# Moving a tiny memory-to-memory transfer from ScalarE's queue into the queue of the loads

## The chip, the cores and the metric

The kernel runs on one core of a Trainium2 chip. The metric is the device time of one execution in microseconds; for the kernel before it is the median of three executions. The profile is a separate execution, and its span runs from the first to the last instruction, so it is a little shorter than the device time. PE is TensorE (PEld its weight loads), DVE is VectorE, ACT is ScalarE, POOL is GpSimd, and SP is SyncE. A name with a q behind it (SPq, ACTq) is that engine issuing a DMA transfer.

## What is computed

```python
def setup_inputs():
    batch, m, k, n = 16, 512, 1024, 768
    return {
        "x": np.random.randn(batch, m, k).astype(np.float32),
        "weight": np.random.randn(k, n).astype(np.float32),
        "sub_value": np.random.randn(batch, m, n).astype(np.float32),
    }

def reference(x, weight, sub_value):
    return (np.matmul(x, weight) - sub_value).astype(np.float32)
```

Batch and m together are 8192 rows, in 64 tiles of 128 rows. The kernel reads x (32 MiB), sub_value (24 MiB) and the weights (3 MiB), and writes the output (24 MiB).

## The kernel before

The kernel is written engine by engine. Each engine has a list of operations (`act.add`, `sp.add`, ...), each with the semaphores that it waits for and the one that it raises; the lists are emitted at the end. For each tile, ScalarE casts x to fp16, TensorE (for most tiles) or VectorE transposes it, ScalarE copies the transposed tile out of PSUM, TensorE multiplies by the weights, and VectorE subtracts sub_value in place, in the ring of buffers from which the output is then stored.

All loads and stores are issued by SP, in a fixed order. A letter names what moves (x, w for weights, s for sub_value, o for output), then come the first tile and the number of tiles:

```python
TRANSFERS = [
    ('x', 0, 1), ('w', 0, 2), ('x', 1, 2), ('w', 2, 2), ('x', 3, 3), ('s', 0, 4),
    ('x', 6, 2), ('x', 8, 4), ('s', 4, 4), ('x', 12, 4), ('s', 8, 8), ('x', 16, 2), ('x', 18, 6), ('s', 16, 8),
    ('x', 24, 8), ('o', 0, 8), ('s', 24, 8), ('x', 32, 8), ('s', 32, 8), ('x', 40, 8),
    # ... cut: the rest alternates in the same way ...
    ('o', 24, 8), ('o', 32, 8), ('s', 56, 8), ('o', 40, 8), ('o', 48, 8), ('o', 56, 5),
    ('o', 61, 2), ('o', 63, 1),
]
```

One more transfer stands outside this list. It copies, from memory to memory, 32 elements (128 bytes) of every 512th row of sub_value into the output, 16 pieces in all. The output's rows are overwritten later by the real stores, so the result does not depend on it. It touches the output's memory early. ScalarE issues it, as the first operation of its list:

```python
    touched = tc.alloc_semaphore("touched")
    act.add(lambda: nc.scalar.dma_start(out=out_flat[:: M_TOT // 16, :Q], in_=sub_flat[:: M_TOT // 16, :Q]), then=(touched, 16))
```

Here `Q` is 32 and `M_TOT` is 8192. The stores wait for it, so that it can't overwrite them, and so in fact does the first of them only (a wait that an engine has made is not repeated):

```python
            if kind == "o":
                waits.append((touched, 16))
                waits.append((counter["finish"], max(finish_at[t] for t in need)))
                # ... cut ...
            sem, value = lane((kind, at))
            # ... cut ...
            if kind == "o":
                here, there = there, here
            sp.add(lambda here=here, there=there: nc.sync.dma_start(out=here, in_=there), waits, (sem, 16))
```

The start of the work, in order, with the parts that the prediction speaks of:

```python
    idle(13)                 # matmuls on zeros, before the first data are there
    cast(0)                  # ACT: waits for x tile 0
    # ... cut: one more idle matmul ...
    transpose_tile(0)        # PE, then ACT copies out of PSUM
    idle(7)
    matmuls(0, 0)            # waits for the first weights, cast by DVE
    matmuls(0, 1)
    idle(2)
    cast(1)
    cast(2)
    # ... cut ...
```

Of the kernel before, what the change touches and what calls it, by code (L numbers as in the profile page):

```python
# [9 lines left out]
Q = 32  # L10
# [94 lines left out]
def kernel(  # L105
# [7 lines left out]
    nc = tc.nc  # L113

    x_flat = x.flatten_outer_dims()
    sub_flat = sub_value.flatten_outer_dims()
    out_flat = out.flatten_outer_dims()

    M_TOT, K = x_flat.shape
# [7 lines left out]
    def view(flat, at, n):  # L127

        first, size = next(one for one in SEGMENTS if one[0] <= at < sum(one))
        assert at + n <= first + size  # L130
        rows = flat[first * P : (first + size) * P].rearrange("(p j) c -> p j c", p=P, j=size)
        return rows[:, at - first : at - first + n]
# [9 lines left out]
    def psum(name, shape, dtype):  # L142
        return ctx.enter_context(nc.psum_tensor(name, shape, dtype)).ap()
# [17 lines left out]
    pt_b = psum("pt_b", [P, NPT, K], F16)  # L161
    po_b = psum("po_b", [P, NPO, 2, 512], F32)

    counter = {}
    for name in ("ident", "idle", "w", "cast", "evac", "pair", "turn", "mul", "finish"):
        counter[name] = tc.alloc_semaphore(name)
# [2 lines left out]
    def count(name):  # L169
        so_far[name] += 1  # L170
        return (counter[name], 1)

    sp, pe = Queue(nc, nc.sync), Queue(nc, nc.tensor)
    act, dve, pool = Queue(nc, nc.scalar), Queue(nc, nc.vector), Queue(nc, nc.gpsimd)

    touched = tc.alloc_semaphore("touched")
    act.add(lambda: nc.scalar.dma_start(out=out_flat[:: M_TOT // 16, :Q], in_=sub_flat[:: M_TOT // 16, :Q]), then=(touched, 16))
    pool.add(lambda: nc.gpsimd.memset(idle_w, 0.0), then=count("idle"))
    pool.add(lambda: nc.gpsimd.memset(idle_x, 0.0), then=count("idle"))  # L179
    dve.add(lambda: nc.vector.memset(ones, 1.0), then=count("ident"))  # L180
# [2 lines left out]
        out=along, data0=ones, data1=ones, initial=0.0, op0=mybir.AluOpType.mult, op1=mybir.AluOpType.add,  # L183
    ), waits=[(counter["ident"], 1)], then=count("ident"))
    dve.add(lambda: nc.vector.transpose(across, along), waits=[(counter["ident"], 3)], then=count("ident"))  # L185
    for a in range(P // Q):
        here = slice(a * Q, (a + 1) * Q)
        dve.add(lambda here=here: nc.vector.tensor_tensor(  # L188
            out=ident[here, here], in0=along[here], in1=across[here], op=mybir.AluOpType.is_equal,
# [41 lines left out]
    def lane(tag):  # L231

        for one in lanes:
            if one["tags"] <= known:
                break
        else:
            one = {"sem": tc.alloc_semaphore(f"lane{len(lanes)}"), "value": 0, "tags": set()}
            lanes.append(one)
        one["value"] += 16
        one["tags"].add(tag)  # L240
        return one["sem"], one["value"]

    def issue():
        nonlocal known, from_w
        while todo:
            kind, at, n = todo[0]
            span = set(range(at, at + n))
            old = {t - NX if kind == "x" else t - NSO for t in span}
            need, by = {
                "w": (set(), "o"),  # L250
                "x": ({t for t in old if t >= 0}, "cast"),
                "s": ({t for t in old if t >= 0}, "o"),
                "o": (span, "finish"),
            }[kind]
            if not need <= done[by]:
                return
            todo.pop(0)
            done[kind] |= span
            if kind == "w":

                first = NSO - 2 * (n_c - at)
                st = so_ring[:, first : first + 2 * n]
                sem, value = lane((kind, at))
                sp.add(lambda st=st, at=at, n=n: nc.sync.dma_start(out=st, in_=w_half[at // n]), then=(sem, 16))  # L264
                for c in range(at, at + n):
                    for r in range(2):
                        here = so_ring[:, first + 2 * (c - at) + r]
                        dve.add(
                            lambda c=c, r=r, here=here: nc.vector.tensor_copy(out=w_sb[:, c, r], in_=here),  # L269
                            waits=[(sem, value)], then=count("w"),  # L270
                        )
                        staged[first + 2 * (c - at) + r] = so_far["w"]
                    w_at[c] = so_far["w"]
                from_w |= {(("w", at), so_far["w"])}
                continue
            ring, size, flat = {
                "x": (x_ring, NX, x_flat), "s": (so_ring, NSO, sub_flat), "o": (so_ring, NSO, out_flat)
            }[kind]
            here = ring[:, at % size : at % size + n]
            there = view(flat, at, n)  # L280
            waits = []
            if kind == "x" and need:
                waits.append((counter["cast"], max(cast_at[t] for t in need)))
                last = max(need, key=lambda t: cast_at[t])
                known |= {tag for t, tag in of_x.items() if t in cast_at and cast_at[t] <= cast_at[last]}
            if kind == "s":
                for t in need:
                    waits.append(landed["o", t])
                    known.add(of_o[t])
                for t in span:  # L290
                    if t % NSO in staged:
                        waits.append((counter["w"], staged.pop(t % NSO)))
                        known |= {tag for tag, value in from_w if value <= waits[-1][1]}
# [3 lines that stand above are left out]
                known |= {of_s[t] for t in finish_at if finish_at[t] <= max(finish_at[u] for u in need)}  # L297
            sem, value = lane((kind, at))
            for t in span:
                landed[kind, t] = (sem, value)  # L300
                {"x": of_x, "s": of_s, "o": of_o}[kind][t] = (kind, at)
            if kind == "o":
                here, there = there, here
            sp.add(lambda here=here, there=there: nc.sync.dma_start(out=here, in_=there), waits, (sem, 16))  # L304

    def cast(mi):
        assert mi in done["x"]
        done["cast"].add(mi)
        x_in = x_ring[:, mi % NX].rearrange("p (g q c r) -> p g c q r", g=2, c=2, r=2)
        first = mi - mi % 2  # L310
        waits = [landed["x", mi]]
        if first in ON_DVE:
            if mi == first:
                b, before = take("x16p", N16P, mi)
                if before is not None:
                    waits.append((counter["pair"], pair_at[before]))
            to = x16p_b[:, slot["x16p", first], mi - first]
        else:
            b, before = take("x16", N16, mi)
            if before is not None:  # L320
                waits.append((counter["turn"], turn_at[before]))
            to = x16_b[:, b]
        to = to.rearrange("p (g c q r) -> p g c q r", g=2, c=2, r=2)
        act.add(lambda: nc.scalar.copy(out=to, in_=x_in), waits, count("cast"))  # L324
        cast_at[mi] = so_far["cast"]
        issue()
# [92 lines left out]
    def finish(mi):  # L419
        assert mi in done["s"]  # L420
        done["finish"].add(mi)
        o = so_ring[:, mi % NSO].rearrange("p (h n) -> p h n", h=2)
        po = po_b[:, slot["po", mi]]
        dve.add(lambda: nc.vector.tensor_tensor(  # L424
            out=o, in0=po[:, :, :NS], in1=o, op=mybir.AluOpType.subtract
        ), [landed["s", mi], (counter["mul"], mul_at[mi])], count("finish"))
        finish_at[mi] = so_far["finish"]
        issue()

    issue()  # L430


# [132 lines left out]
```

## Time and profile before

| | before |
|---|---|
| device time, median of three | 210.57 us (210.28 to 210.61) |
| span of the profiled execution | 208.7 us |
| TensorE busy | 195.2 us (94%) |
| VectorE busy | 127.7 us (61%) |
| ScalarE busy | 113.1 us (54%) |
| bytes moved by DMA | 87.08 MB, 417 GB/s over the span |
| mean granted TensorE clock | 0.993 |

The page cuts the span into 40 slices of about 5.2 us. In the rows of engines and of DMA each digit is the busy share of a slice in tenths, and 9 stands for 90% or more. The row of GB/s says what the DMA engines moved in each slice:

```profile
PEclk9999999999999999999999999999999999999997
GB/s 219 427 426 433 429 433 434 459 426 413 433 466 421 360 438 452 448 408 426 473 408 422 443 419 429 449 438 432 416 454 408 426 452 415 429 438 448 411 412 120
```

In the timeline, a row has the start in us, the duration in us, the engine, the line of the kernel, the operation, and what is written from what; in brackets stands how long the engine had been idle before it and what ended that. A transfer's own row gives the time of its issue on the engine; its time to landing, from issue until its semaphore is complete, stands in the table of transfers.

### The profile page before, as it was taken

The numbers are of one execution on the slowest core, as the hardware profiler recorded it, in microseconds if no ns is written. First come the engines' busy times: TensorE is split into PE (matmuls) and PEld (weight loads), VectorE is DVE, ScalarE is ACT, GpSimd is POOL, SyncE is SP. The second block draws the span as 40 slices with busy tenths as digits, with TensorE's granted clock in tenths as the row PEclk, the third lists the DMA queues.
The fourth block names the chain that finished last, engine by engine and source line by source line (L and its number), as shares of the span: only waits on it lengthen the run. The fifth ranks groups of instructions, "written<-read, shape, count | busy, mean of one in ns | idle before, by whom it ended". The sixth has DMA issues, their size and how long they took to land.

```text
span 208.7 us, 2605 instructions
## 1 busy us (share of the span) xinstructions
PE 195.2 (94%) x1231; PEld 75.4 (36%) x699; DVE 127.7 (61%) x224; ACT 113.1 (54%) x113; POOL 1.0 (0%) x7
## 2 busy tenths in 40 slices
PE   6789799998999999999999999999999999999950
PEld 0133344333434434433442443343344344344310
DVE  2321517945893895597399389479749938942330
ACT  3275678606674761953845676283674747616300
POOL 1000000000000000000000000000000000000000
PEclk9999999999999999999999999999999999999997
DMA  6999999999999999999999999999999999999992
GB/s 219 427 426 433 429 433 434 459 426 413 433 466 421 360 438 452 448 408 426 473 408 422 443 419 429 449 438 432 416 454 408 426 452 415 429 438 448 411 412 120
DMA packets 4932, 87.08 MB, mean 417 GB/s; under 512 B 576, under 2 KB 576, under 8 KB 960
## 3 DMA queue, kind: packets, MB, share of 16 engines
q1 hardware_dynamic: 4896, 87.03, 97.7%
q8 instruction: 1, 0.02, 0.0%
q14 instruction: 3, 0.02, 0.0%
q10 hardware_dynamic: 32, 0.00, 0.0%
HBM read 61.87 MB, written 25.17 MB: 417 GB/s over the span
## 4 chain that ended last, share of the span: by engine, by line
PE 72%; DMA 22%; ACT 2%; issue 1%; DVE 0%; SPq 0%
PE po_b L199 64%; DMA x_ring<-in_x_dram 22%; PE pt_b L342 7%; ACT x_b L324 1%; DVE so_ring L424 0%; ACT xt_b L355 0%; SPq L264 0%; SPq L304 0%; SPq L560 0%; ACT x16p_b L324 0%; SPq L137 0%
## 5 line engine op out<-in xcount | busy, mean ns | idle before, releaser
L199 PE MATMUL po_b<-w_sb,xt_b 128*128 128x384 f16 x704 | 126.0, 326 | 3.2 <-DVE w_sb L269 1.3
L424 DVE TENSOR_TENSOR so_ring<-po_b,so_ring 128x768 f32<-128x768 f32 x64 | 60.5, 956 | 60.0 <-PE po_b L199 38.6
L355 ACT COPY xt_b<-pt_b 128x1024 f16<-128x1024 f16 x44 | 44.5, 1013 | 57.2 <-PE pt_b L342 57.2
L375 DVE STREAM_TRANSPOSE xtp_b<-x16p_b 32x256 f32<-32x256 f32 x144 | 62.7, 435 | 3.5 <-ACT x16p_b L324 1.4
L199 PE MATMUL po_b<-w_sb,xtp_b 128*128 128x384 f16 x320 | 61.4, 326 | 0.5 <-DVE so_ring L424 0.2
L404 PEld LDWEIGHTS <-xt_b 128*128 128x128 f16 x352 | 34.4, 98 | 60.3 <-issue 54.8
L324 ACT CAST x_b<-x_ring 128x1024 f16<-128x1024 f32 x46 | 50.5, 1126 | 9.7 <-DMA x_ring<-in_x_dram 9.7
L342 PE MATMUL pt_b<-ident,x_b 128*128 128x128 f32 x184 | 47.6, 274 | 0.8 <-ACT x_b L324 0.7
L342 PEld LDWEIGHTS pt_b<-ident,x_b 128*128 128x128 f32 x184 | 25.3, 141 | 44.0 <-issue 35.0
L324 ACT CAST x16p_b<-x_ring 128x1024 f16<-128x1024 f32 x18 | 20.3, 1128 | 14.0 <-DMA x_ring<-in_x_dram 14.0
L404 PEld LDWEIGHTS <-xtp_b 128*128 128x128 f16 x160 | 15.7, 98 | 19.2 <-issue 17.1
L269 DVE CAST w_sb<-so_ring 128x768 f16<-128x768 f32 x8 | 3.9, 555 | 9.9 <-DMA so_ring<-in_weight_dram 9.9
L199 PE MATMUL po_b<-idle_x,idle_w 128*128 128x512 f16 x23 | 6.8, 448 | 1.7 <-POOL idle_x L179 1.7
L355 ACT COPY xtp_b<-pt_b 128x1024 f16<-128x1024 f16 x2 | 2.0, 1020 | 1.7 <-PE pt_b L342 1.7
L324 ACT ACT_TABLE_LOAD x1 | 1.3, 1283 | 1.5 <-SPq L137 1.5
L434 PEld LDWEIGHTS <-idle_w 128*128 128x128 f16 x3 | 0.3, 99 | 1.9 <-POOL idle_x L179 1.7
L188 DVE TENSOR_TENSOR ident<-along,across 32x32 f32<-32x32 f32 x4 | 0.7, 183 | 0.1
L180 DVE MEMSET ones<- 128x32 f32 x1 | 0.1, 85 | 1.0 <-SPq L137 1.0
L179 POOL MEMSET idle_x<- 128x512 f16 x1 | 0.5, 529 | 0.0
L506 ACT CAST stub<-ident 128x1 f16<-128x1 f32 x2 | 0.4, 212 | 0.0
L185 DVE STREAM_TRANSPOSE across<-along 128x32 f32<-128x32 f32 x1 | 0.2, 212 | 0.0
L483 POOL MEMSET mark<- 128x1 f32 x1 | 0.1, 99 | 24.2 <-ACT xtp_b L355 24.2
(7 smaller groups left out, 1.0 us busy)
## 6 DMA issues: line engine op xcount, KB each, us to landing
so_ring<-in_sub_value_dram SPq DMA_DIRECT2D x7, 3072.0 KB, 24.2
out_dram<-so_ring SPq DMA_DIRECT2D x7, 3072.0 KB, 26.9
x_ring<-in_x_dram SPq DMA_DIRECT2D x5, 4096.0 KB, 23.5
x_ring<-in_x_dram SPq DMA_DIRECT2D x2, 2048.0 KB, 29.1
so_ring<-in_weight_dram SPq DMA_DIRECT2D x2, 1536.0 KB, 9.5
x_ring<-in_x_dram SPq DMA_DIRECT2D x3, 1024.0 KB, 20.3
so_ring<-in_sub_value_dram SPq DMA_DIRECT2D x2, 1536.0 KB, 23.1
x_ring<-in_x_dram SPq DMA_DIRECT2D x1, 3072.0 KB, 28.0
```

What stands on the lines that cost most here:

```text
L179: pool.add(lambda: nc.gpsimd.memset(idle_x, 0.0), then=count("idle"))
L188: dve.add(lambda here=here: nc.vector.tensor_tensor(out=ident[here, here], in0=along[here], in1=across[here], op=mybir.AluOpType.is_equal, ...
L199: return nc.tensor.add_instruction(mybir.InstMatmult(name=nc.get_next_instruction_name(), engine=full.engine, ins=list(full.ins), outs=lis ...
L269: lambda c=c, r=r, here=here: nc.vector.tensor_copy(out=w_sb[:, c, r], in_=here),
L324: act.add(lambda: nc.scalar.copy(out=to, in_=x_in), waits, count("cast"))
L342: pe.add(lambda: nc.tensor.transpose(words, from_, ident), waits, count("turn") if last else None)
L355: act.add(lambda: nc.scalar.copy(out=to, in_=pt_b[:, b]), waits, count("evac"))
L375: dve.add(lambda: nc.vector.transpose(xt[b * Q : (b + 1) * Q, :, a * Q : (a + 1) * Q], x16[a * Q : (a + 1) * Q, :, b * Q : (b + 1) * Q],), ...
L404: pe.add(lambda weights=weights: nc.tensor.ldweights(weights, tile_position=(0, 0)), [w for w in waits if w[0] in ready])
L424: dve.add(lambda: nc.vector.tensor_tensor(out=o, in0=po[:, :, :NS], in1=o, op=mybir.AluOpType.subtract), [landed["s", mi], (counter["mul"] ...
L434: pe.add(lambda: nc.tensor.ldweights(idle_w, tile_position=(0, 0)), [(counter["idle"], 2)])
L506: lambda t=t: nc.scalar.copy(out=stub[:, t - n_mt : t - n_mt + 1], in_=ident[:, :1]), [(counter["ident"], made)], count("cast")
```

## The change

SP issues the tiny transfer, second in its list, directly behind the load of x tile 0 and ahead of the first weights. ScalarE no longer issues any transfer. The pieces are of 128 elements, 512 bytes, where they were of 32 elements, 128 bytes. There are still 16 of them, in the same rows, and the first store still waits for them. The change is meant to take the issue off ScalarE, to do without a second DMA queue[...].

```diff
+    touched = tc.alloc_semaphore("touched")
     counter = {}
     for name in ("ident", "idle", "w", "cast", "evac", "pair", "turn", "mul", "finish"):
@@
-    touched = tc.alloc_semaphore("touched")
-    act.add(lambda: nc.scalar.dma_start(out=out_flat[:: M_TOT // 16, :Q], in_=sub_flat[:: M_TOT // 16, :Q]), then=(touched, 16))
     pool.add(lambda: nc.gpsimd.memset(idle_w, 0.0), then=count("idle"))
@@
             sp.add(lambda here=here, there=there: nc.sync.dma_start(out=here, in_=there), waits, (sem, 16))
+            if (kind, at) == ('x', 0):
+                sp.add(lambda: nc.sync.dma_start(out=out_flat[:: M_TOT // 16, : 4 * Q], in_=sub_flat[:: M_TOT // 16, : 4 * Q]), [], (touched, 16))
```

The order of the instructions is otherwise the same on every engine.

## The prediction

> **What bounds the kernel now.** I read four views in this order: the forty slices of the page (is anything idle?), the table of windows (which resource is full in which stretch, and when it starts and stops), the timeline of the first five microseconds (where the changed transfer stands), and the transfers with their times to landing.
>
> The slices first. The DMA row is a 9 in every slice but the first and the last; the PE row is the same but for the first three and the last. Two resources are full together, so the chain of waits, which goes through whichever ended last, is not enough to say which one sets the end:
>
> ```profile
> PE   6789799998999999999999999999999999999950
> DMA  6999999999999999999999999999999999999992
> q1 hardware_dynamic: 4896, 87.03, 97.7%
> q10 hardware_dynamic: 32, 0.00, 0.0%
> PE 72%; DMA 22%; ACT 2%; issue 1%; DVE 0%; SPq 0%
> ```
>
> q1 is the loads' and stores' queue on SP, q10 the ScalarE queue that the tiny transfer alone uses: 32 packets, 0.0% of the engines' time.
>
> The windows decide it (columns: window, its length, busy time of PE, PEld, DVE, ACT, POOL with instruction counts, granted clock, DMA share, GB/s):
>
> ```profile
> 2.00:2.25 0.25, 0.25 (x2) 0.00 (x0) 0.22 (x2) 0.25 (x1) 0.00 (x0) 1.00 1.91 197
> 2.25:2.50 0.25, 0.25 (x3) 0.00 (x0) 0.19 (x2) 0.25 (x1) 0.00 (x0) 1.00 0.28 82
> 2.50:2.75 0.25, 0.25 (x2) 0.00 (x0) 0.00 (x0) 0.25 (x1) 0.00 (x0) 1.00 0.52 131
> 2.75:3.00 0.25, 0.25 (x2) 0.00 (x0) 0.00 (x0) 0.07 (x1) 0.00 (x0) 1.00 0.76 246
> 3.00:3.25 0.25, 0.25 (x2) 0.00 (x0) 0.00 (x0) 0.00 (x0) 0.00 (x0) 1.00 1.15 426
> ...
> 2.00:204.50 202.50, 194.84 (x1231) 75.31 (x698) 126.82 (x219) 112.66 (x113) 0.10 (x1) 1.00 1.00 429
> 201.00:204.75 3.75, 0.34 (x3) 0.00 (x0) 0.96 (x1) 0.00 (x0) 0.00 (x0) 1.00 0.93 388
> 204.75:207.25 2.50, 0.00 (x0) 0.00 (x0) 0.00 (x0) 0.00 (x0) 0.00 (x0) 0.70 0.14 55
> ```
>
> From 2.00 to 204.50 us the DMA share is 1.00 at 429 GB/s: 202.5 us x 429 GB/s = 86.9 of the 87.03 MB. So the end is the start of the stream (about 2.0 us, with a ramp until 3.0), plus the bytes over the rate, plus what trails after 204.75, where 55 GB/s are two engines' worth of the sixteen or fewer, plus 1.4 us of closing. PE ends at 201.3, and the last 384 KB are issued at 202.36 into engines that are still busy until 204.75. A change can move the end only by the start of the stream, by time on the 16 engines, by a hole in the stream, or by the trailing engine. PE follows the stream in the opening stretch (24.00 us, busy 18.76 us: it waits for loads) and has almost no idle later.
>
> The start, from the timeline:
>
> ```profile
> 0.90 0.61 ACTq L177 DMA_DIRECT2D out_dram<-in_sub_value_dram  x1
> 0.94 0.38 SPq L304 DMA_DIRECT2D x_ring<-in_x_dram  x1
> 1.37 0.43 SPq L264 DMA_DIRECT2D so_ring<-in_weight_dram  x1
> 1.54 1.28 ACT L324 ACT_TABLE_LOAD   x1 [1.54 <-SPq L137]
> 1.85 0.43 SPq L304 DMA_DIRECT2D x_ring<-in_x_dram  x1
> 4.55 1.11 ACT L324 CAST x_b<-x_ring 128x1024 f16<-128x1024 f32 x1 [1.73 <-DMA x_ring<-in_x_dram]
> 8.30 1.97 DVE L269 CAST w_sb<-so_ring 128x768 f16<-128x768 f32 x4 [5.83 <-DMA so_ring<-in_weight_dram]
> ```
>
> The reader should see that ScalarE, after its issue and its table load, still waits 1.73 us for tile 0, and that VectorE waits for the first weights until 8.30. Both wait for data and not for an issue. And the two transfers in question, from the table of transfers:
>
> ```profile
> x_ring<-in_x_dram SPq DMA_DIRECT2D x1, 512.0 KB, 3.6
> out_dram<-in_sub_value_dram ACTq DMA_DIRECT2D x1, 2.0 KB, 3.8
> ```
>
> 2 KB land 3.8 us after their issue, no sooner than 512 KB. The trace's single packet records tell why: the first packet of tile 0 starts at 1.98 us, and the first q10 packet only at 3.77 us, just behind the semaphore write of tile 0 (3.765). The last engine reaches that point at 4.19. On each engine the tiny packet runs between tile 0 and the first weights already, although it was issued 0.04 us before tile 0 on another queue.
>
> **What the Trainium skill says.** "DMA: Bandwidth & Descriptors", section "Issuing engines are not separate DMA queues": transfers from different issuing engines run on the same 16 DMA engines, and another issuer saves only the time of the sequencer. The trace agrees: the tiny transfer got no engine of its own and waited 2.9 us from issue for tile 0 to drain. Same page, "Queues, rings and completion order": an engine takes one ring in order, pipelined, and goes round the rings it has work for. The trace shows the 12288-byte weight packets starting at 3.785 us, 15 ns after the first tiny one; that they would do so from one ring is what the page says and no run here shows yet. Same page, "Specifications": below 512 bytes the engine does a read-modify-write, which is the reason for pieces of 512 bytes. The trace shows no cost worth saving: a 128-byte packet took 13 ns, and the tiny transfer's sixteen engines had landed between 4.27 and 4.73 us, some 0.5 us after their packets, against 0.34 us for tile 0.
>
> **The change part by part.**
>
> 1. Removed: the issue on ScalarE, 0.61 us. The table load can begin near 0.93 instead of 1.54 and end near 2.2 instead of 2.82. The cast of tile 0 starts when tile 0 lands (4.53, cast at 4.55), so its wait grows from 1.73 to about 2.3 us. On the path: 0.
>
> 2. Added: one issue on SP, between tile 0 and the first weights. The issues of that stretch lie 0.43 to 0.48 us apart; ScalarE's own took 0.61. I take 0.47. The first weights are then issued at 1.84 instead of 1.37. Tile 0 took 1.98 - 0.94 = 1.04 us from issue to first packet; the same gives weights ready at 1.84 + 1.04 = 2.88 (3.02 if the issue costs 0.61). The engines need them when tile 0 drains, 3.77 at the earliest. Margin 0.75 us or more, so no hole. Later issues are more comfortable still: the eleventh transfer, issued at 5.76, is not served until the one before it has landed on most engines at 37.4, and the twelfth waits for ScalarE until 11.86. On the path: 0.
>
> 3. Moved and enlarged: sixteen pieces of 512 instead of 128 bytes, one on each engine. From the packet records, 3072 bytes take 121 ns and 4096 take 159, so 0.037 ns a byte; 384 bytes more make 14 ns, about 27 ns a packet with its 13 ns base. This lies on the path, since every engine is full: +0.014 us. The 6 KB more that are moved are in this.
>
> 4. What waits for the transfer: only the first store, issued at 55.09 us. The transfer had landed at 4.73 us and will land within a few tenths of that. On the path: 0.
>
> The sum is 0.00 + 0.00 + 0.014 + 0.00: 210.57 + 0.01 = 210.58 us. I lower it to 210.5 for the small share I give to a gain in the ramp (second rival).
>
> **The rivals.**
>
> *The tiny transfer holds up the ring.* It is a memory-to-memory copy, with a write to an output that nothing has touched. If in one ring the weights' packets could not pass until it had landed, the stream would lose, on each engine, the time from packet to landing, 0.5 us, up to the 0.96 us between 3.77 and 4.73. All later landings shift: 211.1 to 211.5. For it: now it stands in the same ring. Against it: packets of the ring right behind it ran 15 ns later, while the tiny write was still out, so the engine itself was not blocked. I give it one chance in ten.
>
> *A gain in the ramp.* Between 2.00 and 3.00 us, the windows give (197 + 82 + 131 + 246)/4 = 164 KB where 429 would fit: 0.62 us lost. If the second queue's descriptors, written at the same time as tile 0's, were part of that, up to half might come back: 210.2 to 210.4. For it: both issues overlap, from 0.94 to 1.32. Against it: no q10 packet runs before 3.77, and tile 0's own first packets explain the ramp, 450 to 975 ns where later ones take 159. Two in ten.
>
> *The trailing engine changes.* After 204.75 us only laggards are at work: the last transfer is landed on half of its engines at 205.18 and on the last at 207.41, 2.2 us later. The trace has the lag grow by steps: a 16 KB packet of an instruction queue (0.93 us, at 34.6) comes before the first landing that is 1.4 us late, and a packet of 32 KB that took 2.51 us instead of 1.21 (at 70.0) before the step to 2.2. The change takes one issue from ScalarE's program and gives SP one, which could move such a fetch by an instruction, hardly to another DMA engine. If a step is missing or one is added, the end moves by 0.7 us, either way. This widens the range and not the centre.
>
> **Range and chances.** The three times before span 0.33 us. Adding the steps of the trailing engine one way, and half of the blocked ring the other, I take 209.8 to 211.2. Two per cent are 4.2 us; nothing above reaches a quarter of that. Faster by over 2%: 0.005; slower: 0.01; within: 0.985.
>
> **What would show it.** q10 gone from the table of queues, and q1 with 32 packets more. The weights' issue near 1.84, the table load near 0.93. Tile 0 landing at 4.5, and the first weights at 8.3, each within 0.1 us: this is the test of steps 2 and 3 and of both first rivals. Weights at 8.8 or later mean a blocked ring or a hole; tile 0 before 4.4 means a gain in the ramp. DMA share 1.00 at 429 GB/s from 2.0 to 204.5 as before. If the time moves by more than 0.5 us with the first weights unmoved, I was wrong about what sets the end, and the trailing engine is the place to look.

## The result, and the profile after

| | before | after |
|---|---|---|
| device time, median | 210.45 us (210.28 to 210.61, 4 runs) | 212.03 us (211.97 to 212.28, 4 runs) |
| ratio to before | | 1.0077, 95% interval 1.0060 to 1.0095 |
| span of the profiled execution | 208.7 us | 210.5 us |

The changed kernel is slower by 1.6 us: within 2%, but outside the range of 209.8 to 211.2. Run again later beside other kernels it took 212.10 us against 210.63 (ratio 1.0069, 1.0049 to 1.0089).

First the page's slices and queues, after:

```profile
DMA  4999999999999999999999999999999999999993
GB/s 153 342 429 434 434 428 428 445 409 453 427 441 433 403 427 425 445 444 414 436 445 420 434 425 425 451 441 409 450 431 428 423 425 439 439 425 434 414 402 137
q1 hardware_dynamic: 4928, 87.04, 97.3%
```

The GB/s row has the loss in its first two slices, 153 and 342, where before they were 219 and 427. From the third slice on it is the row of before. q10 is gone and q1 has its 32 packets, as foretold. The timeline of SP and of ScalarE's table load, after (start, duration, engine):

```profile
0.90 1.28 ACT L325 ACT_TABLE_LOAD   x1 [0.90 <-SPq L137]
0.95 0.38 SPq L303 DMA_DIRECT2D x_ring<-in_x_dram  x1
1.39 0.61 SPq L305 DMA_DIRECT2D out_dram<-in_sub_value_dram  x1
2.04 0.57 SPq L263 DMA_DIRECT2D so_ring<-in_weight_dram  x1
2.65 0.43 SPq L303 DMA_DIRECT2D x_ring<-in_x_dram  x1
...
4.72 1.10 ACT L325 CAST x_b<-x_ring 128x1024 f16<-128x1024 f32 x1 [2.54 <-DMA x_ring<-in_x_dram]
...
10.66 1.97 DVE L268 CAST w_sb<-so_ring 128x768 f16<-128x768 f32 x4 [8.19 <-DMA so_ring<-in_weight_dram]
```

Tile 0 is cast at 4.72, 0.17 us later than before. The weights, issued 0.67 us later, are cast at 10.66 where it was 8.30: 2.36 us later. Between an issue that is 0.67 late and data that are 2.36 late lies the riddle of this change. The windows, after (last two columns: DMA share and GB/s):

```profile
3.75:4.25 0.50, 0.50 (x3) 0.00 (x0) 0.00 (x0) 0.00 (x0) 0.00 (x0) 1.00 0.80 240
4.25:4.75 0.50, 0.50 (x3) 0.00 (x0) 0.00 (x0) 0.03 (x1) 0.00 (x0) 1.00 0.36 150
4.75:5.25 0.50, 0.50 (x3) 0.00 (x0) 0.00 (x0) 0.50 (x1) 0.00 (x0) 1.00 0.74 270
5.25:7.25 2.00, 2.00 (x12) 0.57 (x5) 0.00 (x0) 0.57 (x1) 0.00 (x0) 1.00 1.06 344
7.25:9.25 2.00, 1.62 (x8) 0.10 (x1) 0.00 (x0) 1.01 (x1) 0.00 (x0) 1.00 0.87 328
3.75:10.25 6.50, 5.12 (x21) 0.67 (x6) 0.00 (x0) 2.11 (x2) 0.00 (x0) 1.00 0.89 312
12.25:50.00 37.75, 35.05 (x214) 14.33 (x126) 18.27 (x31) 22.23 (x22) 0.10 (x1) 0.95 1.02 433
...
201.00:204.75 3.75, 2.65 (x17) 0.69 (x7) 1.92 (x2) 0.00 (x0) 0.00 (x0) 1.00 0.95 402
204.75:207.25 2.50, 0.00 (x0) 0.00 (x0) 0.00 (x0) 0.00 (x0) 0.00 (x0) 1.00 0.73 299
```

and the same stretches of the kernel before:

```profile
4.25:4.75 0.50, 0.50 (x4) 0.00 (x0) 0.00 (x0) 0.20 (x1) 0.00 (x0) 1.00 0.99 418
3.75:10.25 6.50, 5.17 (x25) 0.86 (x8) 1.95 (x4) 2.12 (x2) 0.00 (x0) 1.00 1.04 435
12.25:50.00 37.75, 35.42 (x225) 14.01 (x132) 18.92 (x31) 21.96 (x23) 0.10 (x1) 1.00 1.01 431
```

This is most of the loss. From 3.75 to 10.25 us the engines moved 312 instead of 435 GB/s: 123 x 6.5 = 800 KB too little, which at 431 GB/s are 1.86 us. From 4.25 us on a third of the engines' rate is at work (150 GB/s, where it was 418), and the rate is full again only after 10 us. The single packet records show what happens there. From 4.4 to 5.1 us seven packets are under way at a time, and sixteen again only from 5.8; in the kernel before it is sixteen throughout. The empty places add up to 13.7 us of one engine, 0.86 us of all sixteen: about half of the loss. The other half lies in packets that take longer, up to 1.5 us where most take 0.46.

Afterwards the rate is the old one and the loss is never made up: the stream is still at 299 GB/s between 204.75 and 207.25, where before it was at 55. (The granted clock is 0.95 instead of 1.00 from 12.25 to 50 us, but the engines move 433 GB/s there, so it does not hold the stream up.)

The late weights come back once more, at the end. TensorE ends at 203.65 instead of 201.34 (its 2.65 us of work after 201.00, against 0.34 in the prediction's window of before), VectorE after it, and so the last store is issued 2.32 us later. Before, the engines had work until 204.75 when it was issued at 202.36; now they run short within half a microsecond of the issue (issue before, then issue and window after):

```profile
202.36 0.33 SPq L304 DMA_DIRECT2D out_dram<-so_ring  x1
```

```profile
204.68 0.33 SPq L303 DMA_DIRECT2D out_dram<-so_ring  x1
...
205.00:205.50 0.50, 0.00 (x0) 0.00 (x0) 0.00 (x0) 0.00 (x0) 0.00 (x0) 1.00 0.38 160
```

This second gap is worth about 0.3 us (5.1 us of one engine in the packet records). The last store lands on the ninth of the sixteen engines at 207.53 instead of 205.18, 2.35 us later, but on the last at 209.22 instead of 207.41, 1.81 us later, because the engine that trails is 1.7 us behind the ninth where it was 2.2. So it is partly chance that the span's growth, 1.8 us, equals the first hole.

### The profile page after: what moved, and what is told of

The parts are those of the page before. It is cut to its first block, busy times and chain, and to the rows that moved or that the text cites. A ratio compares the mean times of both kernels' runs of the same rounds, so it can differ in the third digit from the quotient of the medians.

```text
span 210.5 us, 2605 instructions
## 1 busy us (share of the span) xinstructions
PE 196.4 (93%) x1231; PEld 76.5 (36%) x699; DVE 128.0 (61%) x224; ACT 113.5 (54%) x113; POOL 1.0 (0%) x7
## 4 chain that ended last, share of the span: by engine, by line
PE 74%; DMA 14%; DVE 6%; SPq 3%; issue 1%; DVEq 0%
PE po_b L198 67%; DMA so_ring<-in_sub_value_dram 14%; PE pt_b L343 7%; DVE xtp_b L376 3%; DVE so_ring L425 2%; SPq L303 2%; SPq L263 0%; SPq L305 0%; SPq L561 0%; DVEq L58 0%; SPq L137 0%
## 5 line engine op out<-in xcount | busy, mean ns | idle before, releaser
L343 PEld LDWEIGHTS pt_b<-ident,x_b 128*128 128x128 f32 x184 | 26.3, 144 | 43.2 <-issue 34.7
L198 PE MATMUL po_b<-idle_x,idle_w 128*128 128x512 f16 x23 | 8.0, 509 | 1.7 <-POOL idle_x L178 1.7
```

Source lines behind the costliest of these rows:

```text
L198: return nc.tensor.add_instruction(mybir.InstMatmult(name=nc.get_next_instruction_name(), engine=full.engine, ins=list(full.ins), outs=lis ...
L343: pe.add(lambda: nc.tensor.transpose(words, from_, ident), waits, count("turn") if last else None)
```

## The experiments

Sixteen runs, of small edits to one kernel or the other. "Cover" below is what stands in the queue ahead of the first weights. Landings are those of the trace's semaphore records: when the ninth of the sixteen DMA engines had delivered its share, and when the last had.

**Is it the size of the pieces?** Two runs change one of the two things at a time. The first puts 128-byte pieces second on SP (changed kernel):

```diff
-    out=out_flat[:: M_TOT // 16, : 4 * Q], in_=sub_flat[:: M_TOT // 16, : 4 * Q]
+    out=out_flat[:: M_TOT // 16, :Q], in_=sub_flat[:: M_TOT // 16, :Q]
```

> The changed kernel, but with pieces of 128 bytes again: only the place of the transfer is changed. If a memory-to-memory transfer in the loads' own queue holds up what stands behind it (first theory), or if its issue makes the first weights' issue too late (second), the time stays near 212.0 us, with the first weights landing near 10.6 us. If the longer pieces do the harm (third), it goes back to 210.5, weights at 8.3.

The second puts 512-byte pieces on ScalarE's queue (the reverse edit in the kernel before).

> The kernel before, with pieces of 512 bytes on ScalarE's queue: only the size is changed. First and second theory: 210.5 us, first weights at 8.3. Third theory (the longer pieces): 212.0.

Measured: 211.73 us (ratio 1.0051, 1.0034 to 1.0067) and 210.63 us (1.0001, 0.9994 to 1.0008); 318 and 432 GB/s from 3.75 to 10.25 us. On the old queue the size costs nothing; the new place alone costs two thirds of the change (0.51 of 0.77%) and makes the hole. Size as the cause of the hole is out; whether it costs something in the new place is taken up at the end of the experiments.

**Is it the missing second queue, or the earlier table load?** The tiny transfer is taken out of the kernel before, with the wait for it; the kernel's output does not need it:

```diff
-    act.add(lambda: nc.scalar.dma_start(out=out_flat[...], in_=sub_flat[...]), then=(touched, 16))
-                waits.append((touched, 16))
```

> The kernel before without the tiny transfer and without the first store's wait for it. ScalarE's table load then starts near 0.9 us as in the changed kernel. First and second theory: first weights at 8.3, and 210.5 us unless the early touch of the output is worth something by itself. If the earlier table load or the absence of a second queue did the harm (fourth theory): first weights near 10.6 and about 212.

Measured: 210.56 us (1.0001, 0.9992 to 1.0010), 430 GB/s in the window, and the table load at 0.90 as in the changed kernel. The fourth theory is out. This run also says that the early touch of the output gains nothing measurable.

**Is lateness alone enough?** The kernel before with the weights' issue held by a wait, the tiny transfer left on ScalarE. The number of identity blocks to wait for sets the delay:

```diff
-    sp.add(lambda ...: nc.sync.dma_start(out=st, in_=w_half[at // n]), then=(sem, 16))
+    sp.add(lambda ...: nc.sync.dma_start(out=st, in_=w_half[at // n]), waits=[(counter["ident"], 6)] if at == 0 else [], then=(sem, 16))
```

> The kernel before, with the tiny transfer on ScalarE's queue, but with the issue of the first weights held on SP until VectorE has made two of the four blocks of the identity, near 2.1 us instead of 1.37 (2.04 in the changed kernel). Only the issue is late. Second theory (the late issue makes the hole): about 212.0, first weights near 10.6. First theory: 210.5, first weights within 0.2 us of 8.3.

> The kernel before with the first weights' issue held until the whole identity is made, near 2.5 us (1.37 in the kernel before, 2.07 where it was held for half of the identity and took 211.7). Late-issue theory: the hole grows by about the 0.43 us of further delay on all engines, 212.1 to 212.8 us. If a late issue only costs a fixed restart on some engines, it stays at 211.7.

> The kernel before with the first weights' issue held until three of the four blocks of the identity are made, so that it ends near 2.61 us, as in the changed kernel; the tiny transfer stays on ScalarE's queue. If lateness is all: about 212.0, as the changed kernel. If the transfer's presence in the loads' queue adds something: 211.7, as with holds to 2.07 and 2.50 us.

> The kernel before with the first weights' issue held only until VectorE has transposed the ramp, near 1.65 us, before the engines start on tile 0 at 1.98. Both forms of the late-issue theory: no hole, 210.5, the same as before.

| weights' issue, start to end | GB/s 3.75 to 10.25 | weights landed: ninth / last engine | time, ratio (interval) |
|---|---|---|---|
| 1.37 to 1.80 (before) | 435 | 8.13 / 8.28 | 210.57 |
| 1.64 to 1.97 (hold, f4) | 434 | 8.10 / 8.77 | 210.69, 1.0005 (0.9996 to 1.0013) |
| 2.07 to 2.40 (hold, e4) | 403 | 8.06 / 10.20 | 211.71, 1.0049 (1.0033 to 1.0064) |
| 2.28 to 2.61 (hold, g1) | 312 | 9.90 / 10.49 | 211.70, 1.0047 (1.0033 to 1.0061) |
| 2.50 to 2.83 (hold, f3) | 360 | 8.88 / 9.77 | 211.67, 1.0045 (1.0027 to 1.0063) |
| 2.04 to 2.61 (changed kernel) | 312 | 9.74 / 10.64 | 212.03, 1.0077 (1.0060 to 1.0095) |

Lateness alone makes the hole. The hold whose issue ends when the changed kernel's does has the same rate and the same landings within 0.2 us, with the tiny transfer on the other queue; its time rose by 0.47%, where the changed kernel's rose by 0.77. Its timeline and windows:

```profile
2.28 0.33 SPq L264 DMA_DIRECT2D so_ring<-in_weight_dram  x1
...
4.25:4.75 0.50, 0.50 (x3) 0.00 (x0) 0.00 (x0) 0.05 (x1) 0.00 (x0) 1.00 0.36 148
5.25:7.25 2.00, 2.00 (x13) 0.57 (x5) 0.00 (x0) 1.06 (x2) 0.00 (x0) 1.00 0.98 326
3.75:10.25 6.50, 4.47 (x21) 0.67 (x6) 0.00 (x0) 2.12 (x2) 0.00 (x0) 1.00 0.88 312
```

The cost does not grow with the delay: it is an edge, somewhere near 2 us, with a step of about 1.1 us behind it. The equal times hide unequal sums, though. In the profiles, one execution each, the hold at 2.28 landed its last store 2.1 us later than before on the ninth engine and 1.1 on the last; the hold at 2.50, with the smaller hole, 1.2 on both. Part of a hole disappears in the lag of the trailing engine. At 2.07 the kernel sits on the edge: its twenty runs went from 210.41 to 213.13, and in the profiled one the ninth engine's weights came on time and the last 1.9 us late. My expectation for the hold to 2.5 us, growth with the delay, was wrong.

**Does a memory-to-memory transfer hold up the queue?** Three runs. It is put third on SP, behind the weights:

```diff
+    # in the branch of the first weights, directly after their issue
+                if at == 0:
+                    sp.add(lambda: nc.sync.dma_start(out=out_flat[...4 * Q], in_=sub_flat[...4 * Q]), [], (touched, 16))
     # and the one behind tile 0 is taken out
```

> The changed kernel with the tiny transfer third on SP, one place later, behind the first weights: they are issued at 1.37 us again, and the second x load is the one that is late. Late-issue theory: no hole, because 1.5 MB of weights stand ahead of the late load; 210.5 us, first weights at 8.3. If a memory-to-memory transfer in the loads' queue holds up what stands behind it, the hole moves behind the weights: first weights at 8.3, but the next x load more than 1 us later than before (10.71), and about 212 us.

Or first, ahead of tile 0:

> The tiny transfer first on SP, ahead of tile 0. Late-issue theory: tile 0 is issued 0.65 us later, the weights follow it at the old distance of 0.43, so the whole stream is only shifted: first weights near 8.95, 211.1 to 211.2 us. Memory-to-memory theory: tile 0 is held up as well, by 1 us or more beyond the shift: 212 us or more.

Or it is second, but a plain load of the same pieces into a buffer:

```diff
-    nc.sync.dma_start(out=out_flat[...], in_=sub_flat[:: M_TOT // 16, : 4 * Q])
+    nc.sync.dma_start(out=probe, in_=sub_flat[:: M_TOT // 16, : 4 * Q])
```

> The changed kernel with the second transfer of SP made a load: the same 16 pieces of 512 bytes, now from memory into a buffer that nothing reads (the output is not touched early). Late-issue theory: the weights are issued just as late, 211.7 to 212.1 us. Memory-to-memory theory: 210.5.

Measured: third, 210.56 us (0.9998, 0.9989 to 1.0007), 429 GB/s, and the next x load landed at 11.20 on its last engine against 10.71. Nothing behind the transfer was held up by a microsecond, so that theory is out. First, 211.39 us (1.0042, 1.0026 to 1.0059): tile 0 is issued at 1.65 and its own issue takes 0.55 instead of 0.38; together 0.7 + 0.17 = 0.87 us, and the weights' ninth engine is later by 0.81. There is no hole behind tile 0 although the weights are issued only at 2.24: the engines themselves start on tile 0 only at 2.84 there. So it is not the time on the clock that counts, but the issue's place against the load ahead.

The plain load, second: 210.77 us (1.0017, 1.0003 to 1.0032), where I had expected 211.7 or more. Its timeline gives the reason:

```profile
1.38 0.42 SPq L306 DMA_DIRECT2D probe<-in_sub_value_dram  x1
1.85 0.41 SPq L264 DMA_DIRECT2D so_ring<-in_weight_dram  x1
```

The issue of a load of sixteen pieces takes 0.42 us and the weights' next to it 0.41. The memory-to-memory copy of the same pieces takes 0.61, and the issue behind it 0.57. The weights' issue ends at 2.26 instead of 2.61, and that is just on the near side of the edge: three of its twenty runs took 212.2 to 212.5 us, the others 210.45 to 211.12. To tell this from the kind of transfer, the weights behind the plain load were held until the third block of the identity:

> The small load second on SP (210.77 without a hold), and the first weights held in the same way, so that their issue ends near 2.61 us. Late-issue theory: the hole returns, 211.5 to 212.1. If only the memory-to-memory kind does harm: 210.8.

Measured: 211.79 us (1.0043, 1.0032 to 1.0054), 286 GB/s, weights at 10.05 and 10.95. With a plain load and the late issue the hole is back. So the hole does not need the copy from memory to memory; the copy brings it about through the time of its issue. Only the part of the change above the holds, taken up below, is left for the kind of transfer.

**Does an early issue, or more cover, cure the changed kernel?** With the tiny transfer second on SP, ScalarE issues the first weights in the place of the transfer that it lost:

```diff
-    sp.add(lambda ...: nc.sync.dma_start(out=st, in_=w_half[at // n]), then=(sem, 16))
+    (act if at == 0 else sp).add(lambda ...: (nc.scalar if at == 0 else nc.sync).dma_start(...), then=(sem, 16))
```

> The changed kernel with its tiny transfer second on SP, but with the first weights issued by ScalarE near 0.9 us, in the place of the transfer that it lost. Late-issue theory: the weights share the engines with tile 0 from the start and nothing runs dry: 210.3 to 210.8. Memory-to-memory theory: what is behind it on SP (the second x load) is held up, but has the weights to cover it: 210.5 too, so this one only tells whether the early issue cures the change.

Measured: 210.64 us (1.0000, 0.9991 to 1.0009), 415 GB/s. The cure works. Tile 0 landed at 9.27 instead of 4.53, because it now shares the engines with the weights, and the time did not move. TensorE made up most of that: it ended at 202.05 instead of 201.34, and these 0.7 us did not reach the end of the kernel.

More cover: the changed kernel with a first load of two tiles, and the control with the same loads and the tiny transfer on ScalarE; then a first load of three tiles.

```diff
-    ('x', 0, 1), ('w', 0, 2), ('x', 1, 2), ('w', 2, 2),
+    ('x', 0, 2), ('w', 0, 2), ('x', 2, 1), ('w', 2, 2),    # g3, and h1 on the kernel before
+    ('x', 0, 3), ('w', 0, 2), ('w', 2, 2),                 # h2
```

> The changed kernel with its tiny transfer second on SP, but with a first load of two x tiles (1 MB) and a third of one tile: the same bytes, and the engines busy 1.2 us longer when the late weights come. Late-issue theory: no hole, DMA at full rate from 3.75 to 10.25 us, and 210.3 to 210.9, although the first weights land near 9.5. Memory-to-memory theory: still 212.

> The kernel before (tiny transfer on ScalarE's queue) with a first load of two x tiles and a third of one. If the shortfall with the longer first load came from the late weights: none here, 430 GB/s from 3.75 to 10.25 us, 210.3 to 210.7 us. If the longer load makes it: about 370 GB/s here too.

> The changed kernel (tiny transfer second on SP) with a first load of three x tiles, then both loads of weights: the engines are busy 2.4 us longer when the late weights come. Lead-time theory: no shortfall, 430 GB/s from 3.75 to 12 us, 210.3 to 210.8. If what counts is that the weights' issue comes after the engines have started on what is ahead: a shortfall behind the first load, near 6.5 to 9 us, in the profile.

Measured: 210.75 us (0.9995, 0.9985 to 1.0006), 210.69 (1.0003, 0.9994 to 1.0012) and 210.67 (1.0001, 0.9992 to 1.0010). The rates of g3, h1 and h2 in turn, one kernel to a fence:

```profile
3.75:10.25 6.50, 4.97 (x21) 0.58 (x6) 0.00 (x0) 3.11 (x3) 0.00 (x0) 1.00 0.98 369
```

```profile
3.75:10.25 6.50, 5.15 (x21) 0.58 (x6) 0.87 (x2) 3.12 (x3) 0.00 (x0) 1.00 1.02 429
```

```profile
3.75:10.25 6.50, 6.06 (x21) 0.58 (x6) 0.00 (x0) 2.41 (x3) 0.00 (x0) 1.00 1.01 429
```

Three tiles of cover, and the weights issued at 2.04 as in the changed kernel: no hole. Two tiles: half a hole, 60 GB/s x 6.5 us = 0.9 us against the control, although the first load kept the engines busy until about 5 us, 2.3 us after the weights' issue had ended. So lead time it is, but a much longer one than I had allowed. That g3 nevertheless took no longer has its reason at the other end: its last store had landed on the ninth engine 0.8 us later than before (206.00 against 205.18), but on the last at 207.31 against 207.41. The ninth engine's loss went into the lag behind it, 1.3 us instead of 2.2. (The records do not name the engines, so whether the trailing one was spared the hole is not shown.)

**The changed kernel again**, for its 0.3 us above the holds (0.6 by the ratios, 1.0077 against 1.0047, since the times of before differed too):

> The changed kernel once more. If the presence of the transfer in the loads' queue costs something beyond the lateness: 212.0 again, above the 211.7 of the holds. If not: within 0.2 us of 211.7.

Measured: 212.10 us, weights at 10.17 and 11.23. The excess over the holds came again. The interval of this run (1.0049 to 1.0089) overlaps that of the hold g1 (1.0033 to 1.0061), that of the first measurement (1.0060 to 1.0095) hardly does. So the excess is probably real: lateness alone is shown to cost 1.0 to 1.1 us of the 1.6, and the rest, 0.3 to 0.6, is not explained. With 128-byte pieces in the same place it was 1.0051, as with the holds, which points to the size in this place but does not show it (its interval reaches from 1.0034 to 1.0067). In the profiles the start of the changed kernel and that of g1 are alike (312 GB/s both), and the last landings differ by 0.7 us (209.22 and 208.54), of which the ninth engine has only 0.24.

## Why the prediction was wrong

- **What sets the end** (start of the stream, bytes over rate, holes, trailing engine): right in the main. A hole of 1.86 us of stream came with a span longer by 1.8. But TensorE was not as far from the end as "engines that are still busy until 204.75" made it look: 2.3 us late, it let them run short a second time. The first weights were named as the test, with 8.8 us or later meaning a blocked ring or a hole; they came at 10.6.
- **Step 1**, ScalarE: right. The table load moved to 0.90, the cast's wait grew from 1.73 to 2.54, and nothing came of it. (The prediction's reading of the PE row passed over a 7 in the fifth slice, an 8 in the tenth and a 5 in the last but one; no step rests on it.)
- **Step 2**, the added issue: this is the step that failed. It had two numbers. The issue was to cost 0.47 us, or 0.61 at worst; it cost 0.61, and made the weights' own issue 0.57 instead of 0.43, so that the latter ended at 2.61 instead of 1.80. That was a small miss. The large one is the sentence that the 1.04 us from issue to first packet, taken from tile 0, "gives weights ready at 1.84 + 1.04 = 2.88 (3.02 if the issue costs 0.61)". That was measured on engines that had nothing to do. In the changed kernel a first engine began weights at 3.68, directly behind the tiny transfer, and six others soon after; but at 4.25 to 5.00 us the rate was 147 to 152 GB/s, a third of full, and the other nine began between 5.1 and 5.8: 3 us or more from issue to data, not 1.04. The margin of 0.75 us was none. Holds of the issue alone reproduce it; an earlier issue, or three tiles of cover, removes it.
- **Step 3**, the larger pieces: right. The packet took 27 ns as worked out, and 512 bytes on the old queue cost nothing measurable. Whether they cost something in the new place stays open.
- **Step 4**, the first store's wait: right; the transfer landed 3.5 us after its issue at 1.39, fifty microseconds before it was needed.
- **The rivals.** The blocked ring had the sign and the place (weights later than 8.8) but not the mechanism: third in the queue, the same copy did not keep the next load from arriving in time, and a late issue makes the hole without it. The gain in the ramp did not come: without any tiny transfer the time was the same. The trailing engine did not make the change, but it decides how much of a hole shows in the time, as the longer first load found.
- **The range** was built from these. The late issue was treated as settled by a margin, and got no rival of its own. It needed one: whether the lead that the first weights have is enough.

The Trainium skill's sentence ("DMA: Bandwidth & Descriptors", section "Issuing engines are not separate DMA queues") that another issuing engine saves only the time of the sequencer agrees with the runs: with the first weights issued by ScalarE, 210.64 us. The sentence adds that this time is usually small relative to the transfer, and I took it for small change. At the start of this stream 0.67 us of it opened a hole of 1.86.

What stays open is why engines that are already at work take so much longer to begin on the next transfer. The runs show that they do, and when; no view tells what they wait for. The trace's packets give a hint only. Nine engines had nothing under way for about a microsecond. And in the changed kernel twelve of the weights' packets took 0.9 to 1.5 us instead of 0.46, most of them near 5.5 or near 7 us, and in the kernel before not one did.

## What to carry to other kernels

Where transfers run back to back from the first to the last microsecond, look at the second and third issue as closely as at the first: a small transfer put between two large loads costs its issue time of lead, and if the next load then comes too late the engines run short for far longer than that. Put anything that is not needed early behind enough megabytes (third in the queue was free here), or on the other issuing engine. A margin against running dry has to be measured on engines that are busy, not taken from the very first transfer.

## What was not expected of the hardware

- The issue of a copy from memory to memory, sixteen pieces on sixteen engines, took 0.61 to 0.63 us, and the next issue on SP took 0.55 to 0.57 (0.81 where ScalarE had issued the weights); the issue of a load of the same sixteen pieces took 0.42, and the next 0.41.
- A delay of the second load's issue was free up to a start at 1.64 us, nearly free at 1.85 (behind the small load), and cost about 1.1 us from 2.07 on, without growing to 2.50. Near the edge the runs of one kernel scatter: 210.41 to 213.13 us.
- Tile 0, the first data that TensorE needs, could land 4.7 us later without a change in the time (210.64 us, ratio 1.0000).
